# Layer 2: query projections moved into the recurrence's flow, low-rank projections beside the values, bonus as a thread

## The chip, the cores and the metric

One core of a Trainium2 chip runs the whole two-layer network in one launch. The metric is the device time of a run in microseconds (us). TensorE (PE) does the matmuls, VectorE (DVE) and ScalarE (ACT) and GpSimd (POOL) the elementwise work, and SyncE (SP) issues all the DMAs from one queue.

## The reference

The network is a backbone over 256 context and 512 latent tokens of width 1024. Layer 1 (mLSTM and GLA heads) and the two ConvFFNs are not touched. Layer 2 is bidirectional RWKV-7 time mixing. Six blends of the input `h` with its shifted version feed six projections; then a recurrence runs over the tokens in both directions, for 16 heads of 64:

```python
def rwkv_project(h, shifted, mu, w_rkv, w0, w1, w2, a0, a1, a2, g1, g2, kvec):
    xx = shifted - h
    xr, xw, xk, xv, xa, xg = (h + xx * mu[i] for i in range(6))
    r = xr @ w_rkv[0]
    k = xk @ w_rkv[1]
    v = xv @ w_rkv[2]
    lw = jnp.einsum("zblr,zrd->zbld", jnp.tanh(jnp.einsum("bld,zdr->zblr", xw, w1)), w2) + w0[:, None, None, :]
    decay = jnp.exp(-jnp.exp(-jax.nn.softplus(-lw.astype(jnp.float32)) - 0.5))
    a = jax.nn.sigmoid(a0 + (xa @ a1) @ a2)
    g = jax.nn.sigmoid(xg @ g1) @ g2
    ...
def step(S, inp):
    rt, wt, kt, vt, kkt, at = inp
    sa = jnp.einsum("bhvk,bhk->bhv", S, -kkt)
    S = S * wt[:, :, None, :] + sa[..., None] * (kkt * at)[:, :, None, :] + vt[..., None] * kt[:, :, None, :]
    return S, jnp.einsum("bhvk,bhk->bhv", S, rt)
def rwkv_out(y, p, kvec, lnx, w_o):
    r, k, v, g = p["r"], p["k"], p["v"], p["g"]
    y = head_layernorm(from_heads(y), lnx[0], lnx[1], RW_HEADS, r.dtype)
    bonus = jnp.sum((r * k * kvec[2]).reshape(...), axis=-1, keepdims=True) * v.reshape(...)
    return ((y + bonus.reshape(bn, L, D)) * g) @ w_o
```

Only the latent tokens leave layer 2, so `r` and `g` are needed for 512 tokens; `k`, `v`, `a` and the decay for all 768.

## The kernel before

The channels lie on the partitions: an activation is eight tiles of 128 x 768 (columns 0 to 255 context, `CT`; 256 to 767 latent). A dense projection of one block of 128 outputs ("unit") takes, for each of the eight input chunks, three matmuls: activations and weights are split into a rounded high part and a rest, and high x high, low x high and high x low are summed. `unit` loads 512 KB of weights (`wraw`), lets ScalarE round them (`whi`), and VectorE or GpSimd subtract (`wlo`). `variant` makes a blend: VectorE `vt = xx * mu + h`, ScalarE the high part, VectorE the rest.

On-chip tiles come from one pool of 41 slots of 128 x 780 (`sl`), the weights from 15 slots, PSUM has eight banks. A scheduler below the kernel takes the instructions by their order in the program, but lets a later one go first when it is ready and a slot is free, and gives every slot and wait.

Layer 2's mixer (`rwkv_mixer`) has two parts. The first is written in a fixed order: the shifted differences `xx` (eight tiles; `hf` holds the input); the values (`first("v", ...)` for units 0 to 3, `rkv(2, ...)` for 4 to 7), with two steps of the decay's low-rank projection (`lowrank(1, ...)`, into `uw`) behind each of the last four; then the queries (`pairs(0, CT)`, `first("r", ...)`, `rkv(0, ...)`), with steps of the low-rank projections of `a` (into `ua`) and of the gate (into `ug`) behind them, as the list `LOWS` says. Values and queries go to DRAM (`dv`, `dq`).

The second part is a planner's order. `flow` runs some hundred generators ("threads") and always advances the one that can start first by the times that `Meter` reckons for each instruction; it knows the engines and the PSUM banks, not the 41 slots. What a generator yields is a wait: a name is another thread's end, `"@2"` two banks. The threads, for each pair `p` of heads and each unit `u = 2p + z` (`z` the direction):

- `kp{p}`: the key projection (`kproj`; its variants by `pairs(2, 0)`, the last use of `xx` and `hf`);
- `shared{p}`: `kk`, `a`, the corrected `k`, stored to DRAM (`dkk`, `dP`); it also loads `r` and `v` and works out the bonus, `dbv`;
- `load{p}`: brings `kk`, `P0`, `P1`, `r` back (waits for the last key projection);
- `decay{u}`, `prep{u}`, `past{u}` (stretches of `rwkv_prep`: the products `T1` of a unit and its `dx` in DRAM), `leaf{u}` (inverse of 16 x 16 blocks on VectorE, there and back through DRAM: `dx`, `dqi`, `q0t`), `feed{u}`, `trans{g}_{u}` (TensorE: the chunks' transition matrices, `pmg`, `pmy`, `pmt`), `rec{u}` (the chain over 12 chunks, `cst`);
- `close{p}`: layer norm, bonus, gate; `wo` and `fill` (the modulation projection of the next blocks, `mfill`) take up gaps.

Of the kernel before, what the change touches and what calls it, by code (L numbers as in the profile page):

```python
# [18 lines left out]
P = 128  # L19
# [217 lines left out]
def flow(meter, threads):  # L237

    done, waiting, ready, engine = {}, {}, [], {}
    for i, (name, g) in enumerate(threads):
        ready.append((0.0, i, name, g, 0))

    def place(g):
        while hasattr(g.gi_yieldfrom, "gi_frame"):
            g = g.gi_yieldfrom
        return g.gi_code.co_name, g.gi_frame.f_lineno if g.gi_frame else 0

    def when(e):  # L250

        return max(e[0], meter.free.get(engine.get(place(e[3])), 0.0)), not e[2].startswith("rec"), e[0], e[1]
    while ready:
        e = min(ready, key=when)
        ready.remove(e)
        t, i, name, g, n = e
        if n:
            b = meter.banks(n)
            if b is None:
                waiting.setdefault("@", []).append(e)  # L260
                continue
            if b > t:
# [36 lines left out]
POST_LAG = 0  # L299
UP_TAGS = ({"C": "CCRR", "L": "LLRR"}, {"L": "LRCR"})  # L300
UP_FIRST = 2
LOWS = (0, 0, 1, 2, 2, 1, 1, 1)
RKV_TAGS = dict(v={"C": "CCRR", "L": "LLRR"}, r={"L": "LL"}, k={"L": "L", "C": "C"})


class Net:
# [971 lines left out]
    def rwkv_mixer(self, hf, xd, norms=None, post=lambda *a: None):  # L1278
# [15 lines left out]
        for seg in (CTX, LAT):  # L1294
            if norms is not None:
                next(norms)
            staggered([enter(j, seg) for j in range(NC)])
        uw, ua, ug = self.sl("uw"), self.sl("ua"), self.sl("ug", LT)
        nc.gpsimd.memset(ua[64:128], 0.0)
        dv = self.dr.tile([P, NC, T], F32, name="dv")  # L1300
        dq = self.dr.tile([P, NC, LT], F32, name="dq")

        def store(p, pst, d, segs):
            o = min(s[0] for s in segs)
# [8 lines left out]
        def pairs(i, o):  # L1313
            vh, vl = self.pairs("v")
            staggered([self.variant(i, j, xx, hf, vh, vl, o, T) for j in range(NC)])
            return vh, vl

        def first(which, n, d, segs, vh, vl):
            tags = RKV_TAGS[which]
            psts = self.proj2([I["rkv"][n, p] for p in range(len(tags["L"]))], vh, vl, segs, tags)  # L1320
            for p, pst in enumerate(psts):
                store(p, pst, d, segs)

        def kproj():
# [4 lines left out]
            for p in range(NC):  # L1329
# [14 lines left out]
        def evac_g(o, w, ps):  # L1344
            nc.scalar.activation(ug, ps, AF.Tanh, scale=0.5)
            nc.vector.tensor_scalar(ug, ug, 0.5, 0.5, op0=ALU.mult, op1=ALU.add)
        first("v", 2, dv, (CTX, LAT), vh, vl)
        low = self.lowrank(1, I["rw1"], xx, hf, SEGS, P, "R", lambda o, w, ps: nc.scalar.activation(uw[:, o:o + w], ps, AF.Tanh))
        for p in range(4, NC):
            rkv(2, p, dv, SEGS, vh, vl)  # L1350
            drain(part(low, 2))
        next(low)
        vh, vl = pairs(0, CT)
        low = [self.lowrank(4, I["ra1"], xx, hf, SEGS, 64, "R", lambda o, w, ps: nc.scalar.copy(ua[0:64, o:o + w], ps)),
               self.lowrank(5, I["rg1"], xx, hf, (LAT,), P, "R", evac_g)]
        first("r", 0, dq, (LAT,), vh, vl)
        for p in range(len(RKV_TAGS["r"]["L"]), NC):
            rkv(0, p, dq, (LAT,), vh, vl)
            for g in low:
                drain(part(g, LOWS[p]))  # L1360
        for g in low:
            next(g)
        dz = self.dr.tile([P, NC, LT], F32, name="dz")
        small = (uw, ua, ug, blk, half)
        st = [dict(dirs=[{}, {}], ys=[None]) for _ in range(NC)]
        zh, zl, y = [None] * NC, [None] * NC, []
        meter = self.nc = Meter(nc)
# [27 lines left out]
        def prep(u):  # L1395
            p, z = divmod(u, 2)
            if u:
                yield f"decay{u - 1}"
            yield f"load{p}"
            yield from self.rwkv_prep(p, z, st[p], uw, half, [f"trans{g}_{u - 3}" for g in range(3)] if u > 2 else [])  # L1400

        def leaf(u):
            yield f"prep{u}"
# [26 lines left out]
        def shared(p):  # L1430
            yield f"kp{p}"
            if p > 1:
                yield f"shared{p - 2}"
            yield from self.rwkv_shared(p, dv, dq, small, st[p])

        def load(p):
            yield f"kp{NC - 1}"
            yield f"shared{p}"
            if p:
                yield f"decay{2 * p - 2}"  # L1440
            if p > 1:
                for g in range(3):
                    yield f"trans{g}_{2 * p - 4}"
            self.rwkv_load(p, dq, st[p])
# [30 lines left out]

        preps = [prep(u) for u in range(2 * NC)]
        threads = [(f"kp{p}", kpart(p)) for p in range(NC)] + [(f"shared{p}", shared(p)) for p in range(NC)]
        for u in range(2 * NC):
            p, z = divmod(u, 2)
            threads += [(f"load{p}", load(p))] if z == 0 else []  # L1480
            threads += [(f"decay{u}", stretch(u, "decay")), (f"prep{u}", stretch(u, "prep", "decay")), (f"past{u}", stretch(u, "past", "prep")), (f"leaf{u}", leaf(u)), (f"feed{u}", feed(u))]
            threads += [(f"values{p}", values(p))] if z == 0 else []
# [3 lines left out]
        flow(meter, threads + [("wo", early()), ("fill", self.mod_fill(1, range(4, 12)))])  # L1486
        self.nc = nc
        ss = self.sums(WO_SUMS)
        xc = self.rload(xd, CT)
# [5 lines left out]
        post(y, H1, xc, ss, zh, zl)()  # L1495
        return zh, zl

    def rwkv_shared(self, p, dv, dq, small, st):


        nc, I = self.nc, self.I
# [59 lines left out]
        r, v = self.sl("r", LT), self.sl("v", LT)  # L1561
        nc.sync.dma_start(r, dq[:, p, :])
        nc.sync.dma_start(v, dv[:, p, CT:T])
# [4 lines left out]
        nc.sync.dma_start(dP[0][B], k[B])  # L1568
        nc.sync.dma_start(dP[1][A], k[A])

        nc.vector.scalar_tensor_tensor(r, r, self.v("kvec", 16 + p, 1), k[:, CT:T], op0=ALU.mult, op1=ALU.mult)
        yield True
        yield "@1"
        pb = self.take("pbo")
# [5 lines left out]
        st["dbv"] = self.dr.tile([P, LT], F32, name=f"dbv{p}")  # L1580
        nc.sync.dma_start(st["dbv"], v)

    def rwkv_load(self, p, dq, st):
# [9 lines left out]
        for n, d, w in (("kk", st["dkk"], T), ("P0", st["dP"][0], T), ("P1", st["dP"][1], T), ("r", dq[:, p, :], LT)):  # L1593
            st[n] = self.sl(n, w)
            nc.sync.dma_start(st[n], d)

# [47 lines left out]
    def rwkv_prep(self, p, z, st, uw, half, room):  # L1644
# [1 line left out]


        nc = self.nc
        P0, P1, kk, r, w2 = (st[n] for n in ("P0", "P1", "kk", "r", "w2"))
# [39 lines left out]
        nc.gpsimd.tensor_tensor(ri[:, :, 64:128], c64(r), eL[:, 4:12, e:e + 64], op=ALU.mult)  # L1689

        G3 = lambda t, g: c64(t)[:, 4 * g:4 * g + 4]
        T1 = []
# [453 lines left out]
```

## Time and profile before

| | us |
|---|---|
| median of 3 runs | 2759.9 (2747.04 to 2769.5) |
| profiled execution, its own time | 2768.18 |
| its span in the profile | 2766.2 |
| mean granted TensorE clock | 0.939 of full speed |
| TensorE busy | 2529.3 (91%) |
| TensorE weight loads busy | 2040.7 (74%) |
| VectorE / ScalarE / GpSimd busy | 1605.3 / 1057.3 / 970.0 |

The profile is a page of totals (busy time of the engines, 40 slices of the span, the DMA queues, the costliest groups of instructions) and views that can be asked of any stretch. A row of a stretch reads: from:to in us, length, then busy time with the count of instructions for PE, PEld (weight loads), DVE, ACT, POOL, then the granted clock, the DMA engines' busy share and GB/s. A group reads: line, engine, operation, output<-inputs, shape, count | busy us, mean ns | idle time of the engine ahead of it and what ended it. Many lines of the flow show as L233, since its helper issues every operation; there one goes by the tiles' names (`pk` keys, `pjL` values and queries, `prL` low-rank, `pbo` bonus, `ps` prep's products).

### The profile page before, as it was taken

The page shows a single profiled execution, that of the slowest core. Times are in us where ns is not written, and L with a number is a line of the kernel's source. Part 1 is how long each engine was busy: PE and PEld are TensorE (multiplying, and loading weights), DVE is VectorE, ACT ScalarE, POOL GpSimd, SP SyncE. Part 2 cuts the span into 40 slices and gives each one's busy share as a digit, 9 for nine tenths or more (in the row PEclk, how much of TensorE's full clock was granted, in tenths as well). Part 3 has the DMA queues.
Part 4 walks back from the last instruction along what each step waited for, and adds up shares of the span by engine and source line. Part 5 has one row for each costly group of instructions (what it writes and reads, how often), then busy time and mean ns, then how long its engine had stood idle before and what let it go on. Part 6 is the DMA issues. An engine that isn't in the chain of part 4 may idle for free. (4 is left out here: it accounts for less than half of the span.)

```text
span 2766.2 us, 47123 instructions
## 1 busy us (share of the span) xinstructions
PE 2529.3 (91%) x18916; PEld 2040.7 (74%) x18916; DVE 1605.3 (58%) x2915; ACT 1057.3 (38%) x2205; POOL 970.0 (35%) x1031
## 2 busy tenths in 40 slices
PE   5889999878899999997989879999999998799998
PEld 2677777767888888886756647576768777678886
DVE  4567757734554464747465374665565554676774
ACT  4543443444333232334343233433443443443332
POOL 2443355444222322246212251322222212344425
PEclk8999999998899999997999989999999998899999
DMA  6221234341212212132234453333322222333323
GB/s 226 73 83 60 70 106 146 99 159 52 78 54 59 87 37 78 54 126 73 90 109 151 153 135 80 89 86 98 86 45 65 47 69 85 107 92 94 90 84 107
DMA packets 195667, 254.57 MB, mean 92 GB/s; under 512 B 112120, under 2 KB 127864, under 8 KB 195448
## 3 DMA queue, kind: packets, MB, share of 16 engines
q1 hardware_dynamic: 195448, 251.56, 30.2%
q8 instruction: 149, 2.44, 0.4%
q14 instruction: 70, 0.57, 0.1%
HBM read 213.61 MB, written 37.89 MB: 91 GB/s over the span
## 5 line engine op out<-in xcount | busy, mean ns | idle before, releaser
L397 POOL TENSOR_TENSOR wlo<-wraw,whi 128x512 fp32r<-128x512 f32 (+1 forms) x393 | 543.2, 1404 | 890.7 <-ACT whi L220 454.8
L1123 DVE SCALAR_TENSOR_TENSOR fa<-pl,vec,fa 128x512 f32<-128x512 f32 x352 | 331.3, 948 | 181.4 <-ACT fa L220 175.0
L233 POOL TENSOR_SCALAR_AFFINE_SELECT T<-T 64x256 f32<-64x256 f32 x192 | 98.3, 514 | 270.9 <-ACT T L233 227.4
L220 ACT CAST whi<-wraw 128x512 fp32r<-128x512 f32 (+1 forms) x288 | 149.3, 581 | 68.0 <-DMA wraw<-in_up 26.2
L396 ACT CAST whi<-wraw 128x512 fp32r<-128x512 f32 x241 | 139.0, 619 | 74.0 <-DMA wraw<-in_wmod 22.2
L397 DVE TENSOR_TENSOR wlo<-wraw,whi 128x512 fp32r<-128x512 f32 x136 | 115.5, 887 | 77.8 <-ACT whi L220 34.0
L220 ACT COPY pl<-pjL 128x512 f32<-128x512 f32 x44 | 25.8, 586 | 339.4 <-PE pjL L412 304.0
L408 PE MATMUL pjL<-zh,whi 128*128 128x512 f32 x320 | 126.2, 394 | 2.2 <-ACT whi L220 2.2
L409 PE MATMUL pjL<-ml,whi 128*128 128x512 f32 x320 | 126.6, 396 | 0.0
L409 PE MATMUL pjL<-zl,whi 128*128 128x512 f32 x320 | 126.3, 395 | 0.0
L412 PE MATMUL pjL<-zh,wlo 128*128 128x512 f32 x320 | 126.1, 394 | 0.1
L408 PE MATMUL pjL<-mh,whi 128*128 128x512 f32 x320 | 126.1, 394 | 0.0
L412 PE MATMUL pjL<-mh,wlo 128*128 128x512 f32 x320 | 126.0, 394 | 0.0
L233 DVE TENSOR_SCALAR SU<-cst,el 64x64 f32<-64x64 f32 x176 | 51.1, 291 | 116.2 <-PE cst L233 113.1
L412 PE MATMUL pdL<-gh,wlo 128*128 128x512 f32 x288 | 113.8, 395 | 1.0 <-POOL wlo L397 1.0
L408 PE MATMUL pdL<-gh,whi 128*128 128x512 f32 x288 | 113.3, 394 | 0.2 <-ACT whi L220 0.2
L409 PE MATMUL pdL<-gl,whi 128*128 128x512 f32 x288 | 113.2, 393 | 0.0
L1175 DVE TENSOR_TENSOR y<-y,pdL 128x512 f32<-128x512 f32 x48 | 33.0, 687 | 108.3 <-PE pdL L412 108.2
L233 PE MATMUL pmy<-T,q0t 64*64 64x192 f32 x768 | 94.1, 349 | 0.8 <-DVE SU L233 0.8
L233 ACT ACTIVATE SU<-cst,el 64x64 f32<-64x64 f32 x176 | 53.6, 307 | 104.1 <-PE cst L233 103.6
L233 PE MATMUL ps<-bk,av 64*64 64x192 f32 x768 | 89.5, 355 | 3.5 <-DVE bk L233 1.9
L408 PE MATMUL pjC<-mh,whi 128*128 128x256 f32 x320 | 89.8, 281 | 0.0
(502 smaller groups left out, 7328.1 us busy)
## 6 DMA issues: line engine op xcount, KB each, us to landing
wraw<-in_up SPq DMA_DIRECT2D x88, 512.0 KB, 3.6
wraw<-in_wmod SPq DMA_DIRECT2D x64, 512.0 KB, 4.0
wfill<-in_wmod SPq DMA_DIRECT2D x32, 512.0 KB, 5.1
wraw<-in_rkv SPq DMA_DIRECT2D x24, 512.0 KB, 3.8
wraw<-in_win_fm SPq DMA_DIRECT2D x21, 512.0 KB, 4.4
wraw<-in_down SPq DMA_DIRECT2D x32, 320.0 KB, 2.9
xd<-y SPq DMA_DIRECT2D x64, 128.0 KB, 1.8
wraw<-in_down SPq DMA_DIRECT2D x32, 256.0 KB, 2.6
```

What stands on the lines that cost most here:

```text
L220: return lambda *a, **k: self.tc.keep_in_program_order(f(*a, **k))
L233: return f(*a, **k)
L396: nc.scalar.copy(hi[:, c], raw[:, c])
L397: (nc.gpsimd if lo == "pool" else nc.vector).tensor_tensor(w[:, c], raw[:, c], hi[:, c].bitcast(F32), op=ALU.subtract)
L408: nc.tensor.matmul(pst[tag][:m, :w], w1, xh[kc][:, o:o + w], start=st, stop=False)
L409: nc.tensor.matmul(pst[tag][:m, :w], w1, xl[kc][:, o:o + w], start=False, stop=False)
L412: nc.tensor.matmul(pst[tag][:m, :w], w0, xh[kc][:, o:o + w], start=False, stop=sp)
L1123: nc.vector.scalar_tensor_tensor(b, src, fw(f, i), b, op0=ALU.mult, op1=ALU.add)
L1175: nc.vector.tensor_tensor(yj, yj, pst[tag][:, :w], op=ALU.add)
```

## The change

- The query stage leaves the fixed order. At the mixer's start, 16 DMAs store the latent columns of `hf` and `xx` in DRAM (`dhx`). In the flow, after the last key projection, two threads (`rvar0`, `rvar1`) load them back a chunk at a time and make the query variants; threads `rp{p}` do the query units, two at a time, and store each in a DRAM tile of its own (`dq[p]`); `rload{p}` brings it back. `prep` takes `r` after its decay part and waits for `rload` there; unit 2's decay waits for the last query unit.
- The gate's low-rank projection becomes a thread, `gates`, after the last query unit, with loads and variants of its own; `close` waits for it.
- The low-rank projection of `a` moves to the values: units 4 and 5 carry four steps each of the decay's, 6 and 7 four steps each of `a`'s.
- The bonus leaves `rwkv_shared` and is a thread, `bonus{p}`, after `prep{2p}`; it loads `r`, `v` and the two halves of `k` from DRAM. `close` waits for it.
- `flow` learns a signal within a thread: a yield of `"!3"` marks the step as done under the thread's name with that mark.

```diff
@@ flow
+        elif isinstance(x, str) and x[0] == "!":
+            done[name + x] = t = max(t, meter.end)
+            ready += [(max(t, t2), *r) for t2, *r in waiting.pop(name + x, ())]
+            ready.append((t, i, name, g, 0))
@@ rwkv_mixer
-        uw, ua, ug = self.sl("uw"), self.sl("ua"), self.sl("ug", LT)
+        dhx = [self.dr.tile([P, 2, LT], F32, name=f"dhx{j}") for j in range(NC)]
+        for j in range(NC):
+            nc.sync.dma_start(dhx[j][:, 0], hf[j][:, CT:T])
+            nc.sync.dma_start(dhx[j][:, 1], xx[j][:, CT:T])
+        uw, ua = self.sl("uw"), self.sl("ua")
...
+        def latent(i, chunks, use):
...
+            for n, j in enumerate(chunks):
+                for e in chunks[n:n + 2]:
+                    if e not in src:
+                        src[e] = self.sl("hx", LT), self.sl("hx", LT)
+                        for q in range(2):
+                            nc.sync.dma_start(src[e][q], dhx[e][:, q])
+                h, x = src[j]
+                hi, lo = self.sl("rh", LT, F32R), self.sl("rl", LT, F32R)
+                yield True
+                nc.vector.scalar_tensor_tensor(x, x, self.v("mu", i * 8 + j, 1), h, op0=ALU.mult, op1=ALU.add)
...
+                nc.scalar.copy(hi, x)
...
+                nc.vector.tensor_tensor(lo, x, hi.bitcast(F32), op=ALU.subtract)
+                yield True
+                use(j, hi, lo)
+                yield f"!{j}"
...
+        def rpart(p, rh, rl, us):
...
+            us[p] = self.unit(I["rkv"][0, p], "pool" if p % 2 else "dve")
+            yield "@1"
+            ps = self.take("pr")
+            for j in range(NC):
+                yield f"rvar{j % 2}!{j}"
+                for k, (a, b) in enumerate(((0, rh), (0, rl), (1, rh))):
+                    nc.tensor.matmul(ps, us[p][a][:, j * P:(j + 1) * P], b[j], start=j + k == 0, stop=j == NC - 1 and k == 2)
+                yield False
...
+            nc.sync.dma_start(dq[p], t)
...
         for p in range(4, NC):
             rkv(2, p, dv, SEGS, vh, vl)
-            drain(part(low, 2))
-        next(low)
-        vh, vl = pairs(0, CT)
...
-        first("r", 0, dq, (LAT,), vh, vl)
-        for p in range(len(RKV_TAGS["r"]["L"]), NC):
-            rkv(0, p, dq, (LAT,), vh, vl)
-            for g in low:
-                drain(part(g, LOWS[p]))
...
+            drain(part(low[(p - 4) // 2], 4))
+            if p % 2:
+                next(low[(p - 4) // 2])
@@ prep
+            if u == 2:
+                yield f"rp{NC - 1}"
             yield f"load{p}"
-            yield from self.rwkv_prep(p, z, st[p], uw, half, [f"trans{g}_{u - 3}" for g in range(3)] if u > 2 else [])
+            yield from self.rwkv_prep(p, z, st[p], uw, half, ([f"trans{g}_{u - 3}" for g in range(3)] if u > 2 else []) + [f"rload{p}"])
@@ threads
+        def queries(p):
+            yield f"kp{NC - 1}"
+            if p > 1:
+                yield f"rp{p - 2}"
+            yield from rpart(p, rh, rl, rus)
+
+        def variants(i):
+            yield f"kp{NC - 1}"
...
+            yield from latent(0, range(i, NC, 2), use)
+
+        def gates():
+            yield f"rp{NC - 1}"
+            yield from gproj()
+
+        def bonus(p):
+            yield f"prep{2 * p}"
+            if p:
+                yield f"bonus{p - 1}"
+            yield from self.rwkv_bonus(p, dv, dq[p], blk, st[p])
...
+        def rload(p):
+            yield f"rp{p}"
+            yield f"load{p}"
+            st[p]["r"] = self.sl("r", LT)
+            self.nc.sync.dma_start(st[p]["r"], dq[p])
+            yield True
...
         def close(p):
             yield f"rec{2 * p + 1}"
+            yield f"bonus{p}"
+            yield "gates"
@@ rwkv_bonus (was in rwkv_shared)
+        r, v, k = (self.sl(n, LT) for n in ("r", "v", "k"))
+        nc.sync.dma_start(r, dq)
+        nc.sync.dma_start(k[A], st["dP"][1][A, CT:T])
+        nc.sync.dma_start(k[B], st["dP"][0][B, CT:T])
+        nc.sync.dma_start(v, dv[:, p, CT:T])
+        yield True
+        nc.vector.scalar_tensor_tensor(r, r, self.v("kvec", 16 + p, 1), k, op0=ALU.mult, op1=ALU.mult)
```

More of the change, by code (lines that the diff above doesn't have):

```diff
@@ L301 @@
 UP_FIRST = 2
-LOWS = (0, 0, 1, 2, 2, 1, 1, 1)
-RKV_TAGS = dict(v={"C": "CCRR", "L": "LLRR"}, r={"L": "LL"}, k={"L": "L", "C": "C"})
+RKV_TAGS = dict(v={"C": "CCRR", "L": "LLRR"})
 class Net:
@@ L1297, in rwkv_mixer @@
             staggered([enter(j, seg) for j in range(NC)])
-        uw, ua, ug = self.sl("uw"), self.sl("ua"), self.sl("ug", LT)
+        dhx = [self.dr.tile([P, 2, LT], F32, name=f"dhx{j}") for j in range(NC)]
[3 more added lines that the diff above has]
+        uw, ua = self.sl("uw"), self.sl("ua")
         nc.gpsimd.memset(ua[64:128], 0.0)
         dv = self.dr.tile([P, NC, T], F32, name="dv")
-        dq = self.dr.tile([P, NC, LT], F32, name="dq")
+        dq = [self.dr.tile([P, LT], F32, name=f"dq{p}") for p in range(NC)]
         def store(p, pst, d, segs):
@@ L1343, in kproj @@
                 yield "next"
-        def evac_g(o, w, ps):
+        def latent(i, chunks, use):
+            nc = self.nc
+            src = {}
+            for n, j in enumerate(chunks):
[15 more added lines that the diff above has]
+                yield f"!{j}"
@@ L1345, in evac_g, with gproj, use @@
+        def gproj():
+            nc = self.nc
+            wg = self.unit(I["rg1"])
+            yield "@1"
+            ps = self.take("prg1")
+            def use(j, hi, lo):
+                for k, (a, b) in enumerate(((0, hi), (0, lo), (1, hi))):
+                    nc.tensor.matmul(ps, wg[a][:, j * P:(j + 1) * P], b, start=j + k == 0, stop=j == NC - 1 and k == 2)
+            yield from latent(5, range(NC), use)
+            yield True
             nc.scalar.activation(ug, ps, AF.Tanh, scale=0.5)
+            self.close(ps)
+            yield True
@@ L1346, in evac_g @@
             nc.vector.tensor_scalar(ug, ug, 0.5, 0.5, op0=ALU.mult, op1=ALU.add)
+        def rpart(p, rh, rl, us):
+            nc = self.nc
+            us[p] = self.unit(I["rkv"][0, p], "pool" if p % 2 else "dve")
+            yield "@1"
+            ps = self.take("pr")
[4 more added lines that the diff above has]
+                yield False
+            yield True
+            t = self.sl("pr", LT)
+            nc.scalar.copy(t, ps)
+            self.close(ps)
+            yield True
+            nc.sync.dma_start(dq[p], t)
@@ L1347, in rwkv_mixer @@
         first("v", 2, dv, (CTX, LAT), vh, vl)
-        low = self.lowrank(1, I["rw1"], xx, hf, SEGS, P, "R", lambda o, w, ps: nc.scalar.activation(uw[:, o:o + w], ps, AF.Tanh))
+        low = [self.lowrank(1, I["rw1"], xx, hf, SEGS, P, "R", lambda o, w, ps: nc.scalar.activation(uw[:, o:o + w], ps, AF.Tanh)),
+               self.lowrank(4, I["ra1"], xx, hf, SEGS, 64, "R", lambda o, w, ps: nc.scalar.copy(ua[0:64, o:o + w], ps))]
         for p in range(4, NC):
             rkv(2, p, dv, SEGS, vh, vl)
-            drain(part(low, 2))
@@ L1352, in rwkv_mixer @@
-        next(low)
-        vh, vl = pairs(0, CT)
-        low = [self.lowrank(4, I["ra1"], xx, hf, SEGS, 64, "R", lambda o, w, ps: nc.scalar.copy(ua[0:64, o:o + w], ps)),
-               self.lowrank(5, I["rg1"], xx, hf, (LAT,), P, "R", evac_g)]
-        first("r", 0, dq, (LAT,), vh, vl)
-        for p in range(len(RKV_TAGS["r"]["L"]), NC):
-            rkv(0, p, dq, (LAT,), vh, vl)
-            for g in low:
-                drain(part(g, LOWS[p]))
-        for g in low:
-            next(g)
+            drain(part(low[(p - 4) // 2], 4))
@@ L1363, in rwkv_mixer @@
+            if p % 2:
+                next(low[(p - 4) // 2])
         dz = self.dr.tile([P, NC, LT], F32, name="dz")
+        ug = self.sl("ug", LT)
         small = (uw, ua, ug, blk, half)
+        rh, rl, rus = [None] * NC, [None] * NC, {}
         st = [dict(dirs=[{}, {}], ys=[None]) for _ in range(NC)]
@@ L1433, in shared, with use @@
                 yield f"shared{p - 2}"
-            yield from self.rwkv_shared(p, dv, dq, small, st[p])
+            yield from self.rwkv_shared(p, small, st[p])
+        def queries(p):
[5 more added lines that the diff above has]
+            yield f"kp{NC - 1}"
+            def use(j, hi, lo):
+                rh[j], rl[j] = hi, lo
+            yield from latent(0, range(i, NC, 2), use)
[7 more added lines that the diff above has]
+            yield from self.rwkv_bonus(p, dv, dq[p], blk, st[p])
         def load(p):
@@ L1443, in load @@
                     yield f"trans{g}_{2 * p - 4}"
-            self.rwkv_load(p, dq, st[p])
+            self.rwkv_load(p, st[p])
+            yield True
+        def rload(p):
[3 more added lines that the diff above has]
+            self.nc.sync.dma_start(st[p]["r"], dq[p])
             yield True
@@ L1477, in rwkv_mixer @@
         threads = [(f"kp{p}", kpart(p)) for p in range(NC)] + [(f"shared{p}", shared(p)) for p in range(NC)]
+        threads += [(f"rvar{i}", variants(i)) for i in range(2)] + [(f"rp{p}", queries(p)) for p in range(NC)]
         for u in range(2 * NC):
             p, z = divmod(u, 2)
-            threads += [(f"load{p}", load(p))] if z == 0 else []
+            threads += [(f"load{p}", load(p)), (f"rload{p}", rload(p))] if z == 0 else []
             threads += [(f"decay{u}", stretch(u, "decay")), (f"prep{u}", stretch(u, "prep", "decay")), (f"past{u}", stretch(u, "past", "prep")), (f"leaf{u}", leaf(u)), (f"feed{u}", feed(u))]
-            threads += [(f"values{p}", values(p))] if z == 0 else []
+            threads += [(f"values{p}", values(p)), (f"bonus{p}", bonus(p))] if z == 0 else []
             threads += [(f"trans{g}_{u}", trans(u, g)) for g in ((0, 1, 2), (0, 2, 1))[z]]
@@ L1485, in rwkv_mixer @@
             threads += [(f"close{p}", close(p))] if z else []
-        flow(meter, threads + [("wo", early()), ("fill", self.mod_fill(1, range(4, 12)))])
+        flow(meter, threads + [("gates", gates()), ("wo", early()), ("fill", self.mod_fill(1, range(4, 12)))])
         self.nc = nc
@@ L1496, in rwkv_mixer, with rwkv_shared @@
         return zh, zl
-    def rwkv_shared(self, p, dv, dq, small, st):
+    def rwkv_shared(self, p, small, st):
         nc, I = self.nc, self.I
@@ L1560, in rwkv_shared @@
         nc.sync.dma_start(dP[1][B], q[B])
-        r, v = self.sl("r", LT), self.sl("v", LT)
-        nc.sync.dma_start(r, dq[:, p, :])
-        nc.sync.dma_start(v, dv[:, p, CT:T])
         nc.vector.tensor_scalar(a, a, -1.0, self.v("kvec", 8 + p, 1), op0=ALU.add, op1=ALU.mult)
@@ L1569, in rwkv_shared, with rwkv_bonus @@
         nc.sync.dma_start(dP[1][A], k[A])
-        nc.vector.scalar_tensor_tensor(r, r, self.v("kvec", 16 + p, 1), k[:, CT:T], op0=ALU.mult, op1=ALU.mult)
+    def rwkv_bonus(self, p, dv, dq, blk, st):
+        nc = self.nc
+        A, B = slice(0, 64), slice(64, 128)
+        r, v, k = (self.sl(n, LT) for n in ("r", "v", "k"))
[3 more added lines that the diff above has]
+        nc.sync.dma_start(v, dv[:, p, CT:T])
+        yield True
+        nc.vector.scalar_tensor_tensor(r, r, self.v("kvec", 16 + p, 1), k, op0=ALU.mult, op1=ALU.mult)
         yield True
@@ L1581, in rwkv_shared, with rwkv_load @@
         nc.sync.dma_start(st["dbv"], v)
-    def rwkv_load(self, p, dq, st):
+    def rwkv_load(self, p, st):
         nc, I = self.nc, self.I
@@ L1592, in rwkv_load @@
         st["w2"] = w2[:, 0], w2[:, 1]
-        for n, d, w in (("kk", st["dkk"], T), ("P0", st["dP"][0], T), ("P1", st["dP"][1], T), ("r", dq[:, p, :], LT)):
+        for n, d, w in (("kk", st["dkk"], T), ("P0", st["dP"][0], T), ("P1", st["dP"][1], T)):
             st[n] = self.sl(n, w)
@@ L1648, in rwkv_prep @@
         nc = self.nc
-        P0, P1, kk, r, w2 = (st[n] for n in ("P0", "P1", "kk", "r", "w2"))
+        P0, P1, kk, w2 = (st[n] for n in ("P0", "P1", "kk", "w2"))
         C6 = math.exp(-0.5)
@@ L1688, in rwkv_prep @@
         nc.vector.scalar_tensor_tensor(av, c64(kk), -1.0, eL[:, :, z:z + 64], op0=ALU.mult, op1=ALU.mult)
-        nc.gpsimd.tensor_tensor(ri[:, :, 64:128], c64(r), eL[:, 4:12, e:e + 64], op=ALU.mult)
+        nc.gpsimd.tensor_tensor(ri[:, :, 64:128], c64(st["r"]), eL[:, 4:12, e:e + 64], op=ALU.mult)
         G3 = lambda t, g: c64(t)[:, 4 * g:4 * g + 4]
```

## The prediction, made before the change was run

> **What bounds the kernel now.** I read the page first (busy shares, the 40 slices), then cut layer 2 into stages with the view that gives busy time by stretches, then looked inside two of them with the groups, the waits and the order of time.
>
> ```profile
> PE 2529.3 (91%) x18916; PEld 2040.7 (74%) x18916; DVE 1605.3 (58%) x2915; ACT 1057.3 (38%) x2205; POOL 970.0 (35%) x1031
> core 0: us, PE busy (x) PEld busy (x) DVE busy (x) ACT busy (x) POOL busy (x), PEclk, DMA share, GB/s
> 1342.00:1386.00 44.00, 42.13 (x239) 36.01 (x237) 20.40 (x22) 16.96 (x30) 12.84 (x9) 1.00 0.42 148
> 1386.00:1459.00 73.00, 65.34 (x268) 44.32 (x267) 44.72 (x56) 29.89 (x50) 9.35 (x7) 1.00 0.33 106
> 1459.00:1575.00 116.00, 112.22 (x594) 83.75 (x592) 46.05 (x68) 34.92 (x60) 35.52 (x28) 0.99 0.42 136
> 1575.00:1670.00 95.00, 69.56 (x481) 42.67 (x480) 68.14 (x164) 28.81 (x57) 42.87 (x67) 0.78 0.62 166
> 1670.00:2320.00 650.00, 626.45 (x8327) 478.56 (x8324) 354.01 (x969) 258.56 (x630) 163.77 (x310) 0.95 0.30 75
> ```
>
> The five rows are the stages the change touches: values 4 to 7 with the decay low-rank projection; queries with the other two low-rank projections; keys (the first part of the planner's flow); the start of the recurrence; its long remainder. TensorE is the busiest engine, and four rows show it full or nearly so. The fourth does not. In those 95 us it is busy 69.6 us, at a granted clock of 0.78, so it does about 69.6 x 0.78 = 54 us of full-clock work: **some 41 us are spare**. Nothing else with so much room is near. Where the hole is:
>
> ```profile
> 1575.00:1585.00 10.00, 5.61 (x19) 1.98 (x17) 5.03 (x6) 3.08 (x6) 3.95 (x5) 0.95 0.88 263
> 1585.00:1595.00 10.00, 4.94 (x6) 1.67 (x6) 5.24 (x8) 1.58 (x2) 1.18 (x1) 0.50 0.93 344
> 1655.00:1665.00 10.00, 2.54 (x18) 2.07 (x19) 7.83 (x31) 0.00 (x0) 2.25 (x5) 0.53 1.11 196
> PE pmg L233 <- DMA q0t<-dqi: 8.8, 1, 8.8
> PE pbo L233 <- DVE r L233: 8.6, 2, 5.4
> 1461.73 0.97 PE L233 MATMUL pk<-vh,whi 128*128 128x512 f32 x4 [0.51 <-ACT vh L233]
> 1573.94 0.52 PE L233 MATMUL pk<-vh,wlo 128*128 128x512 f32 x2
> 1662.46 0.45 PE L233 MATMUL pmg<-q0t,T 64*64 64x64 f32 x2 [8.80 <-DMA q0t<-dqi]
> 1592.06 1.18 POOL L233 TENSOR_TENSOR ri<-r,eL 128x512 f32<-128x512 f32 x1 [13.11 <-ACT eL L233]
> ```
>
> The keys run from 1461.7 to 1574.4; then two pieces follow. When the last key projection ends, everything runs on loads (DMA 0.9 busy) and on the bonus's `r`; later the first `trans` waits for the leaf inverse's trip through DRAM. Both are latency: a chain load, prep, T1, leaf, q0t that nothing shortens, with too little TensorE work beside it: 88 us from the last key matmul to the first `trans`. The change brings TensorE work (the query projections) to exactly this stretch, so the question is how much of it fits.
>
> **The change part by part, on the profiled execution (2768.2 us).** The shown runs' median, 2759.9 us, is 8.3 us below it, inside their spread; I carry the difference over.
>
> *The query stage goes from the fixed order.* Its contents:
>
> ```profile
> L408 PE MATMUL pjL<-vh,whi 128*128 128x512 f32 x48 | 19.0, 397 | 0.5 <-ACT pv L1307 0.5
> L435 PE MATMUL pjL<-vl,whi 128*128 128x512 f32 x16 | 7.1, 446 | 0.3 <-DVE vl L1254 0.3
> L409 PE MATMUL prL<-rl,whi 128*128 128x512 f32 x8 | 3.8, 473 | 1.4 <-DVE rl L1254 1.4
> L409 PE MATMUL prL<-rl,whi 128*64 128x512 f32 x8 | 3.3, 412 | 3.0 <-DVE rl L1254 3.0
> 1430.73 0.39 PE L408 MATMUL prL<-rh,whi 128*128 128x512 f32 x1
> 1430.96 0.40 PE L408 MATMUL pjL<-vh,whi 128*128 128x512 f32 x1
> 1431.19 0.39 PE L409 MATMUL pjL<-vl,whi 128*128 128x512 f32 x1
> ```
>
> Each group has two sisters (high x high, low x high, high x low), so queries are 3 x (48 + 16) = 192 matmuls of 512 columns, the gate projection 24, the `a` projection 24 plus 24 of 256 columns. The starts in order of time are 0.23 us apart though each lasts 0.39 (they overlap), so I count 0.233 us a piece: queries 44.7 us, gate 5.6, `a` 5.6 + 2.8 = 8.4. Together 58.7 of the stage's 73, the rest is waiting for variants. Term: **-73.0**.
>
> *The `a` projection moves beside the values.* +8.4 us on TensorE. The values' stretch then carries 16 low-rank steps for 8; the query stage lost 73 - 58.7 = 14.3 us over its entry and 16 steps, under 0.9 a step, so eight more cost 0 to 7; I take 4, since the values' stretch with its eight steps lost only 1.9 us. **+12.4**. The keys' entry is as before: their variants wait for the last projection's slots in both orders.
>
> *Queries and gates in the flow.* 44.7 + 5.6 = **+50.3** on TensorE if nothing hides. The spare 41 us of the hole take most: **-40.7**. But the work isn't there at once. Their input is now 16 loads of 256 KB (16 more for the gates), variants are computed again, and `r` goes out and back:
>
> ```profile
> L1251 DVE SCALAR_TENSOR_TENSOR vt<-xx,vec,y 128x512 f32<-128x512 f32 x15 | 12.1, 808 | 1.3 <-DMA dq<-pv 1.1
> L1252 ACT CAST vh<-vt 128x512 fp32r<-128x512 f32 x8 | 4.9, 618 | 8.9 <-DVE vt L1251 8.9
> L1254 DVE TENSOR_TENSOR vl<-vt,vh 128x512 fp32r<-128x512 f32 x8 | 5.5, 691 | 6.1 <-ACT vh L1252 6.1
> L397 DVE TENSOR_TENSOR wlo<-wraw,whi 128x512 fp32r<-128x512 f32 x4 | 2.6, 687 | 5.9 <-DMA dq<-pv 5.9
> r<-dq SPq DMA_DIRECT2D x16, 256.0 KB, 4.6
> dq<-pv SPq DMA_DIRECT2D x8, 256.0 KB, 3.6
> ```
>
> The first variant is ready 4.6 + 0.81 + 0.62 + 0.69 = 6.7 us after its loads are issued, and they are issued when the last key projection frees the bank of slots; eight need 8 x (0.81 + 0.69) = 12 us of VectorE. Query 0 is thus done some 25 us into the stretch (6.7, the 12, and a share of VectorE's other work: an estimate), and reaches prep 0 about 3.6 + 4.6 us and a copy (0.6) later. Its `ri` now waits that long (before: 18 us in); the trip is hidden from TensorE by queries 1 to 7 (39 us of matmuls), not from the chain. VectorE carries 68 us in 95 already and gets 12 of variants and 4 x 2 x 0.69 = 5.5 of weight halves: still under its span. Then slots: 41 tiles, of which query variants hold 16 and `uw`, `ua`, `ug`, `zero` 4, so unit 1's preparation comes behind query 7 and the second hole (7.5 us idle, the rest at 0.53) stays in part. Not hidden: 6.7 at the head, and about 15 near the first `trans`, twice that hole's idle: **+22**. Ends: 0, if loads and variants are hoisted into the key stage, and 41, if nothing fits.
>
> *Bonus a thread.* Its work (2 matmuls, two VectorE passes a pair) leaves the start and comes later, with four loads and one store a pair.
>
> ```profile
> L233 PE MATMUL pbo<-r,blk 128*128 128x512 f32 x8 | 6.1, 878 | 8.6 <-DVE r L233 8.6
> L233 PE MATMUL mfill<-wfill,cth 128*2 128x512 f32 x23 | 12.1, 633 | 0.0
> ```
>
> On TensorE 16 matmuls, at most 2 x 6.1 = 12 us; the remainder has 650 - 626 x 0.95 = 55 us spare and takes them: 0, up to +12 if that cover is gone. The modulation filler (23 in the hole) is off the path: displaced pieces go to later gaps; up to +12 if none takes them. So -6 (a lighter start) to +24 for both, I take 0, the row nearest being the 55 spare.
>
> *Sixteen stores of the two inputs.* They are issued when the shifted input is done:
>
> ```profile
> 1310.00:1320.00 10.00, 2.58 (x6) 1.95 (x7) 10.00 (x14) 3.38 (x6) 6.90 (x7) 0.50 0.00 0
> 1330.00:1340.00 10.00, 10.00 (x45) 8.17 (x44) 0.04 (x1) 0.70 (x2) 0.00 (x0) 1.00 0.00 0
> dbv<-v SPq DMA_DIRECT2D x8, 256.0 KB, 2.0
> ```
>
> The DMA engines do nothing there and the values' first weights are in: 4 MB at the 344 GB/s seen above is 12 us of an empty queue. 0; were the stores to block SP ahead of the next weights, up to +6.
>
> **Sum:** -73.0 + 12.4 + 50.3 - 40.7 + 22 = **-29.0**: 2739 for the profiled execution, 2731 against the median.
>
> **Rivals.**
>
> *Nothing fits (2760).* The query threads begin only after the last key; they delay prep 0 as much as they fill, and the spare time is still there behind them. Then -73 + 12.4 + 50.3 + 8.8 for the trip of `r` = -1.5. For it: the 16 + 8 slots, VectorE at 72% in the hole. Against: queries 1 to 7 need no answer from anybody.
>
> *It fits altogether (2709).* The 22 us left are taken by the key stage (early loads) and by the remainder: -51.
>
> ```profile
> PE cst L233 <- DVE SU L233: 10.5, 19, 2.1
> ```
>
> For it: the remainder's 55 us, of which TensorE's waits (the longest group above) are only part. The Trainium skill ("Perfetto Trace Analysis", Identifying the Most-Contended Engine) says that matmul occupancy is no good measure of TensorE's headroom and that the weight loads' busy share is better; by that rule the remainder has room for another 25%, not 4%, and all the moved work could hide there. The trace has 479 of 650 us for weight loads, but no row shows which of the two is right. Against: the matmuls there are small and many, and no wait is long.
>
> *Slower: the SP queue (2793).* SP issues in order, and the remainder hangs on it:
>
> ```profile
> 1642.72 0.45 SPq L233 DMA_DIRECT2D dqi<-leaf  x1
> 1649.26 5.32 SPq L233 DMA_DIRECT2D dx<-T  x6
> 1656.55 2.62 SPq L233 DMA_DIRECT2D q0t<-dqi  x2
> ```
>
> `q0t` left 13.8 us after the store it depends on, behind `dx` stores that waited for ScalarE, and `trans` paid 8.8. Now the bonus's store (which waits VectorE, TensorE and a slot) and its loads, `r`'s load and the gates' 16 loads stand in that queue in every pair. Where one is ahead of `q0t` or `kk`, `P0`, the pair pays up to 8.8 us: from 4 pairs on (35 us) the gain is gone, at 7 (62) it is -29 + 62 = +33. For it: the slots are scarcer too. Against: TensorE's longest waits in the remainder are the recurrence's own steps (the row above), not a DMA.
>
> **How the numbers follow.** Forecast 0.45 (own range 2711 to 2751), nothing fits 0.22, altogether 0.15, slower 0.18. The range takes the whole forecast, the second, most of the third and half of the last: 2702 to 2788, with some 0.15 to 0.2 outside. About 1% (27.6 us) is what a measurement of this kernel can tell from no change, and the forecast lies on that line: 0.24 of it faster, 0.21 same. Faster 0.24 + 0.15 = 0.39; same 0.21 + 0.18 + 0.03 = 0.42; slower 0.04 + 0.15 = 0.19.
>
> **What would show it.** Keys begin about 60 us sooner (near 1401 for 1461) with the values' stretch some 12 us longer; `pr` matmuls at 0.23 apart from some 7 us behind the last `pk`, done within 60 us; first `pmg` after the last `pk` by 88 us (as now) to 110; granted clock over that stretch nearer 0.95 than 0.78; remainder near 650 us plus what gates and bonus add, with no DMA among TensorE's waits. **Wrong** would be made by: a clock still near 0.8 there (nothing fits); `q0t` or `r` among TensorE's longest waits (the queue); keys that start less than 50 us sooner, since the values' stretch then is bound by its 16 variants.

## The result, and the profile after

| | before | after |
|---|---|---|
| median | 2760.3 us (2747.0 to 2769.5) | 2734.4 us (2730.8 to 2738.1) |
| ratio to before | | 0.9904, 95% interval 0.9881 to 0.9926 |
| span of the profiled execution | 2766.2 | 2732.7 |

The changed kernel is faster by 26.5 us (20 to 33); the forecast was 2731. The profiled executions differ by 33.5 us, of which 6.6 arose ahead of the mixer: its first shifted input stands at 1277.0 before and at 1270.4 after, and in the fourteen traces of this case, with the same work ahead of it, that row lies anywhere from 1267.9 to 1277.0. Times inside the mixer are therefore given from that row on.

The tile views give, for each group of TensorE or GpSimd instructions, count, then duration min/median/max in ns, then start of the first and of the last. Of the kernel before (last keys, first `trans` and the last product of the output projection):

```profile
L1219 POOL TENSOR_TENSOR xx<-y x16: 603/925/1332, 1277.0 to 1315.0; 128x255 f32<-128x255 f32 x8, 128x504 f32<-128x504 f32 x4, 128x448 f32<-128x448 f32 x4
L233 PE MATMUL pk<-vh,wlo x128: 274/389/629, 1464.0 to 1574.2; 128*128 128x512 f32 x64, 128*128 128x256 f32 x64
L233 PE MATMUL pmg<-q0t,T x768: 216/218/367, 1662.5 to 2264.8; 64*64 64x64 f32 x192
L233 PE MATMUL wo<-zh,wlo x48: 387/396/628, 2254.5 to 2319.1; 128*128 128x512 f32 x48
```

And of the changed kernel, with the query units (`pr`):

```profile
L1222 POOL TENSOR_TENSOR xx<-y x16: 606/924/1336, 1270.4 to 1308.5; 128x255 f32<-128x255 f32 x8, 128x504 f32<-128x504 f32 x4, 128x448 f32<-128x448 f32 x4
L233 PE MATMUL pk<-vh,whi x128: 275/387/988, 1394.8 to 1500.5; 128*128 128x512 f32 x64, 128*128 128x256 f32 x64
L233 PE MATMUL pk<-vh,wlo x128: 274/387/628, 1397.1 to 1501.0; 128*128 128x512 f32 x64, 128*128 128x256 f32 x64
L233 PE MATMUL pr<-rh,wlo x64: 387/393/794, 1512.1 to 1619.3; 128*128 128x512 f32 x64
L233 PE MATMUL pmg<-q0t,T x768: 216/218/367, 1584.6 to 2225.9; 64*64 64x64 f32 x192
L233 PE MATMUL wo<-zh,wlo x48: 387/397/503, 2212.9 to 2283.1; 128*128 128x512 f32 x48
```

| from the first shifted input | before | after | change |
|---|---|---|---|
| first key matmul | 184.7 | 124.4 | -60.3 |
| last key matmul | 297.2 | 230.6 | -66.6 |
| first `trans` | 385.5 | 314.2 | -71.3 |
| last output product | 1042.1 | 1012.7 | -29.4 |

So 71 us are gained by the first `trans`, and 42 of them are given back behind it. The stages (columns as before: from:to, length, busy us of PE, PEld, DVE, ACT, POOL, granted clock, DMA share, GB/s):

```profile
1394.00:1501.00 107.00, 104.16 (x587) 83.36 (x586) 46.03 (x68) 37.63 (x65) 38.04 (x25) 0.98 0.42 129
1501.00:1585.00 84.00, 78.33 (x449) 51.80 (x448) 46.97 (x105) 29.89 (x56) 31.91 (x49) 0.95 0.68 203
1585.00:1630.00 45.00, 43.02 (x441) 29.88 (x440) 13.04 (x35) 12.17 (x26) 3.33 (x3) 0.86 0.39 121
1630.00:1710.00 80.00, 76.78 (x774) 49.56 (x774) 63.37 (x149) 37.04 (x86) 38.62 (x68) 0.98 0.45 121
1710.00:2285.00 575.00, 551.48 (x7371) 421.63 (x7370) 325.21 (x887) 227.15 (x554) 143.96 (x268) 0.96 0.34 87
PE pr L233 <- DVE rl L233: 3.0, 2, 2.9
PE mfill L233 <- ACT frow L233: 1.3, 2, 0.7
PE pmg L233 <- DVE leaf L233: 1.3, 1, 1.3
```

The hole is closed: 84 us from the keys to the first `trans` where it was 88, TensorE busy 78 of them at a clock of 0.95, spare 84 - 78.3 x 0.95 = 9.6 us. (The 95 us and the 41 spare of the prediction are of a stretch that runs 7.5 us past the first `trans`; from 1574 to 1662.5 TensorE was busy 63.1 us at 0.81, which leaves 37 spare.) The three last rows are TensorE's longest waits between 1501 and 1630; the 8.8 us on `q0t` are gone. That looks like a plain success of filling, and the experiments show that it isn't one.

### The profile page after: what moved, and what is told of

It reads as the page before. It is cut to its first block, busy times and chain, and to the rows that moved or that the text cites. A ratio compares the mean times of both kernels' runs of the same rounds, so it can differ in the third digit from the quotient of the medians.

```text
span 2732.7 us, 47246 instructions
## 1 busy us (share of the span) xinstructions
PE 2517.5 (92%) x18916; PEld 2031.1 (74%) x18916; DVE 1594.9 (58%) x2915; ACT 1056.1 (39%) x2205; POOL 974.7 (36%) x1031
## 5 line engine op out<-in xcount | busy, mean ns | idle before, releaser
L400 POOL TENSOR_TENSOR wlo<-wraw,whi 128x512 fp32r<-128x512 f32 (+1 forms) x383 | 528.5, 1402 | 836.9 <-ACT whi L220 468.5
L399 ACT CAST whi<-wraw 128x512 fp32r<-128x512 f32 x223 | 128.1, 618 | 56.7 <-DMA wraw<-in_wmod 24.2
L400 DVE TENSOR_TENSOR wlo<-wraw,whi 128x512 fp32r<-128x512 f32 x128 | 109.2, 891 | 65.5 <-ACT whi L220 34.3
L233 POOL TENSOR_TENSOR wlo<-wraw,whi 128x512 fp32r<-128x512 f32 (+1 forms) x26 | 34.7, 1348 | 158.1 <-ACT whi L233 121.7
```

The lines of the kernel that those rows point to most:

```text
L233: return f(*a, **k)
L399: nc.scalar.copy(hi[:, c], raw[:, c])
L400: (nc.gpsimd if lo == "pool" else nc.vector).tensor_tensor(w[:, c], raw[:, c], hi[:, c].bitcast(F32), op=ALU.subtract)
```

## The experiments

All ratios are to the kernel before, run on the same chip (medians 2759.7, 2762.5 and 2760.0 in the three groups of four). One per cent is 27.6 us.

| run | median us | ratio | 95% interval |
|---|---|---|---|
| the changed kernel | 2734.4 | 0.9904 | 0.9881 to 0.9926 |
| e1 queries in the fixed order | 2756.5 | 0.9991 | 0.9978 to 1.0004 |
| e2 no queries | 2693.5 | 0.9760 | 0.9747 to 0.9773 |
| e3 no gates | 2724.3 | 0.9869 | 0.9857 to 0.9882 |
| e4 before, `a` beside the values | 2765.5 | 1.0017 | 0.9998 to 1.0036 |
| e5 unit 2 without its wait | 2749.4 | 0.9958 | 0.9944 to 0.9972 |
| e6 queries preferred | 2726.4 | 0.9871 | 0.9852 to 0.9890 |
| e7 gates beside the values | 2726.5 | 0.9874 | 0.9854 to 0.9893 |
| e8 before, bonus a thread | 2760.0 | 0.9990 | 0.9975 to 1.0005 |
| e9 few query matmuls | 2735.4 | 0.9910 | 0.9878 to 0.9942 |
| e10 one variant pair | 2741.7 | 0.9934 | 0.9916 to 0.9952 |
| e11 e6 and e7 together | 2726.9 | 0.9875 | 0.9851 to 0.9899 |
| e12 e11, variants earlier | 2724.7 | 0.9873 | 0.9850 to 0.9896 |

**Which part of the change is it?** e1 undoes the queries' move alone:

```diff
...
+        vh, vl = pairs(0, CT)
+        first("r", 0, dq, (LAT,), vh, vl)
+        for p in range(2, NC):
+            rkv(0, p, dq, (LAT,), vh, vl)
         dz = self.dr.tile([P, NC, LT], F32, name="dz")
...
-            yield from rpart(p, rh, rl, rus)
+            return
...
-            yield from latent(0, range(i, NC, 2), use)
+            return
+            yield
```

> The query units go back to the fixed order behind the values (their variants from the on-chip input); gates, bonus and the a projection stay as in the changed kernel. Theory (the gain is TensorE work of the queries hidden in the start of the recurrence): the stage costs 44.7 us of matmuls and 4 to 5 of entry again, and the flow gives back the some 23 it pays for them, so about 2760 (2752 to 2767), with the stretch from the last key matmul to the first trans at a granted clock near 0.8 again. Rival (the gain comes from the other moves: a beside the values, bonus and gates out of the way): 2734, within 6.

It came out at 2756.5: nothing that can be told from the kernel before is left of the gain. In its trace the query stage is back, and so is the hole, with its clock:

```profile
1384.00:1447.00 63.00, 57.77 (x230) 38.57 (x228) 21.28 (x30) 22.60 (x40) 10.88 (x9) 1.00 0.42 135
1553.00:1647.00 94.00, 68.28 (x427) 40.23 (x425) 67.85 (x161) 31.42 (x59) 42.81 (x62) 0.83 0.65 177
```

The other moves were put on the kernel before one at a time. e4 gives the values the steps of both low-rank projections:

```diff
         for p in range(4, NC):
             rkv(2, p, dv, SEGS, vh, vl)
-            drain(part(low, 2))
-        next(low)
+            drain(part(low[(p - 4) // 2], 4))
+            if p % 2:
+                next(low[(p - 4) // 2])
...
```

> The kernel before, with only the a projection moved beside the values; queries and the gate's projection stay in the fixed order. Theory: TensorE work only changes places, and 8 waits of under 0.9 us become 8 of about half: 2757 (2750 to 2762). Rival (the low-rank projections behind the queries were the stall, and this move is the gain): 2745 or less.

e8 takes the bonus out of `rwkv_shared` into its thread:

```diff
+        def bonus(p):
+            yield f"prep{2 * p}"
+            if p:
+                yield f"bonus{p - 1}"
+            yield from self.rwkv_bonus(p, dv, dq[:, p, :], blk, st[p])
...
             yield f"rec{2 * p + 1}"
+            yield f"bonus{p}"
...
```

> The kernel before with only the bonus made a thread. Theory: its work moves out of the stretch between the keys and the first trans, which waits on loads anyway, into the remainder, which has room: 2758 (2750 to 2766). Rival (its waits on loads at the start were part of the hole): 2750 or less.

Neither moves the time beyond the noise: +4.7 us (-0.6 to +9.9) and -2.8 us (-6.9 to +1.4). So the gain belongs to the queries' move. What each way of doing them costs is seen against a kernel without them, e2:

```diff
...
-            yield from rpart(p, rh, rl, rus)
+            return
...
+        for d in dq:
+            nc.sync.dma_start(d, zero[:, 0:LT])
...
```

> The query units and their variants are left out (r is zero, stored once); everything else as in the changed kernel. Theory: only the part of the queries that isn't hidden goes, some 23 us: 2711 (2702 to 2718). Rival (nothing of them is hidden, they only changed places): their 44.7 us of matmuls and more go, 2688 or less.

2693.5: **the queries cost 63 us in the fixed order (2756.5 - 2693.5) and 40 us in the flow (0.9904 - 0.9760 = 1.44%)**, with 44.7 us of matmuls in both. Here the theory's number, 23, failed, and the time fell between the two that were expected: next to nothing of the 44.7 is hidden in the flow. What the move saved is mainly the rest of the fixed stage, some 18 us beyond its matmuls. Yet e2's trace has the same hole, open:

```profile
1499.00:1591.00 92.00, 68.32 (x426) 40.18 (x424) 67.88 (x160) 31.43 (x59) 42.07 (x62) 0.82 0.67 179
1591.00:1640.00 49.00, 49.00 (x659) 36.73 (x660) 20.03 (x45) 18.98 (x45) 9.66 (x19) 0.92 0.39 97
```

Its first `trans` comes 92 us behind the last key, the changed kernel's 84 us, so the queries don't delay it. But the two stretches don't hold the same work. From the last key to the first `trans` TensorE runs, in e2 (first row) and in the changed kernel:

```profile
L233 PE MATMUL ps<-ri,bk 64*64 64x128 f32 x96 | 6.6, 288 | 0.0
L233 PE MATMUL ps<-ri,bk 64*64 64x128 f32 x64 | 3.8, 269 | 0.0
L233 PE MATMUL pr<-rh,whi 128*128 128x512 f32 x48 | 19.9, 436 | 0.0
```

A unit has 32 of the first kind. e2, like the kernel before, has made the products of three units by its first `trans`, the changed kernel of two. Its 144 query matmuls (the last row and two sisters) took in part the place of the third unit, which comes behind.

**Is unit 2's wait the price?** The third `ri` (the step of `prep` that uses `r`) shows when the third unit is made; the GpSimd rows in order of time, of e2:

```profile
1517.40 1.18 POOL L233 TENSOR_TENSOR ri<-r,eL 128x512 f32<-128x512 f32 x1
1538.73 1.18 POOL L233 TENSOR_TENSOR ri<-r,eL 128x512 f32<-128x512 f32 x1
1560.72 1.56 POOL L233 TENSOR_TENSOR ri<-r,eL 128x512 f32<-128x512 f32 x1 [0.39 <-POOL T L233]
```

and of the changed kernel:

```profile
1544.81 1.18 POOL L233 TENSOR_TENSOR ri<-r,eL 128x512 f32<-128x512 f32 x1
1552.16 1.73 POOL L233 TENSOR_TENSOR ri<-r,eL 128x512 f32<-128x512 f32 x1
1639.50 1.70 POOL L233 TENSOR_TENSOR ri<-r,eL 128x512 f32<-128x512 f32 x1 [1.02 <-ACT eL L233]
```

Counted from the last key matmul (1498.9 and 1501.0) the third unit is 77 us later, behind the last query (1619). e5 takes the wait out:

```diff
-            if u == 2:
-                yield f"rp{NC - 1}"
```

> The changed kernel, but unit 2's decay doesn't wait for the last query unit (its load and slots still gate it). Theory (the queries are free up to the first trans, and then cost some 30 us because unit 2, which starts 64 us later than in the run without queries, leaves the recurrence without its third unit): unit 2's first matmul comes before 1600 us, the third rec ends 15 to 25 us sooner, and the time falls by 8 to 20: 2720. Rival (the 41 slots, not the wait, hold unit 2 back: 16 are the query variants'): no change within 5, or slower.

The kernel became slower by 15 us. In its profiled execution (2760.3 us, the slowest of ten) the third `ri` came 72 us behind the last key instead of 138, the first `trans` 96 us instead of 84. SP waited for the leaf inverse's tiles 37.5 us in the stretch from 1500 to 1720, where the changed kernel has 11.7:

```profile
SPq L233 <- DVE leaf L233: 37.5, 8, 14.5
SPq L233 <- DVE leaf L233: 11.7, 6, 8.4
```

(the second row is the changed kernel's). So the wait isn't a fault. That it keeps a third unit off the tiles and the queue that the first two need is the likely reason, not a shown one: e2 has its third unit as early, and SP waits there 18.7 us. e6 moves the end of the queries instead: the planner prefers them.

```diff
-        return max(e[0], meter.free.get(engine.get(place(e[3])), 0.0)), not e[2].startswith("rec"), e[0], e[1]
+        return max(e[0], meter.free.get(engine.get(place(e[3])), 0.0)), not e[2].startswith(("rec", "rp", "rvar")), e[0], e[1]
```

> The changed kernel, but the planner prefers the query threads, as it does the recurrence's chain, where two could start at once; so the queries end sooner and units 0 and 1 are made later. Theory (unit 2's late start is the price): the last query matmul comes 20 us or more before 1619, unit 2 follows, and the time falls by 5 to 15: 2724. Rival (the price is TensorE time, which only changes hands): within 5 of 2734; if the first trans is later by as much as the queries are sooner, slower by up to 10.

2726.4, faster by about 9 us (0.9871 against 0.9904, the intervals overlap a little). Counted from the last key, the last query matmul came 48 us sooner (71 for 118) and the third unit's `ri` 37 us sooner (102 for 138), but the first `trans` 36 us later (120 for 84). Shifts of that size come down to 9 at the end. So the third unit's place is not the price by itself: 72 us behind the last key in e5, 102 in e6 and 138 in the changed kernel went with 2749, 2726 and 2734.

**TensorE's time, or what surrounds it?** e9 keeps everything of the queries but the matmuls, of which a few small ones remain; e10 keeps all the matmuls and takes away 14 of the 16 slots, 14 loads and seven variants.

```diff
-                for k, (a, b) in enumerate(((0, rh), (0, rl), (1, rh))):
-                    nc.tensor.matmul(ps, us[p][a][:, j * P:(j + 1) * P], b[j], start=j + k == 0, stop=j == NC - 1 and k == 2)
+                for k, (a, b) in enumerate(((0, rh), (0, rl))[:1 + (p == NC - 1)]):
+                    nc.tensor.matmul(ps[:, :128], us[p][a][:, j * P:(j + 1) * P], b[j][:, :128], start=j + k == 0, stop=j == NC - 1 and k == (p == NC - 1))
...
```

> The changed kernel with its loads, variants, weights, copies and slots, but of a query unit's 24 matmuls of 512 columns only 8 of 128 columns are left (16 in the last unit); r is wrong. Theory (what the queries still cost in the flow, 41 us by the run without them, is TensorE's time: the idle time that they fill comes back further on): nearly all of it goes, 2700 (2693 to 2708). Rival (the price is what surrounds them: 16 slots, loads, VectorE, the late r): 2718 or more.

```diff
-                yield f"rvar{j % 2}!{j}"
+                yield "rvar0!0"
...
-                    nc.tensor.matmul(ps, us[p][a][:, j * P:(j + 1) * P], b[j], start=j + k == 0, stop=j == NC - 1 and k == 2)
+                    nc.tensor.matmul(ps, us[p][a][:, j * P:(j + 1) * P], b[0], start=j + k == 0, stop=j == NC - 1 and k == 2)
...
-            yield from latent(0, range(i, NC, 2), use)
+            yield from latent(0, range(1 - i), use)
```

> The changed kernel with all its query matmuls, but all read one pair of variant tiles, made from one chunk (14 loads, 7 variants and 14 slots fewer); r is wrong. Theory (TensorE's time): 2730 (2722 to 2736). Rival (the slots and the loads): 2715 or less.

Neither gave anything: e9's 2735.4 agrees with its rival, e10's 2741.7 lies above what its theory and its rival expected. With 120 of 192 query matmuls gone and the other 72 at 128 columns for 512, the time is the changed kernel's. In e9's stretch behind the keys the hole is open again and TensorE idle, to no avail (first two rows); in e10 TensorE is full there (third row), the first `trans` is the earliest of all with queries in the flow, 73 us behind the last key, and the end isn't earlier:

```profile
1500.00:1595.00 95.00, 71.60 (x418) 46.84 (x416) 62.94 (x118) 37.84 (x70) 45.76 (x58) 0.80 0.73 220
1595.00:1640.00 45.00, 41.38 (x543) 32.22 (x545) 21.95 (x54) 16.29 (x38) 7.47 (x19) 0.89 0.52 125
1500.00:1595.00 95.00, 93.75 (x671) 63.91 (x672) 50.69 (x118) 32.33 (x62) 35.55 (x49) 1.00 0.57 163
```

What e9 does and doesn't show is seen in the whole stretch from the last key to the last output product, of e2, the changed kernel and e9:

```profile
1498.90:2247.00 748.10, 705.90 (x8824) 524.74 (x8823) 435.95 (x1151) 292.19 (x693) 209.46 (x374) 0.94 0.38 98
1501.00:2283.10 782.10, 747.71 (x9016) 551.02 (x9015) 448.08 (x1171) 305.34 (x719) 217.82 (x387) 0.95 0.39 105
1505.50:2285.30 779.80, 723.11 (x8896) 537.69 (x8895) 451.59 (x1171) 305.60 (x717) 222.57 (x383) 0.93 0.40 104
```

The changed kernel takes 34 us more than e2, with TensorE 42 us busier and 8 us less idle: the moved matmuls lengthen the flow by nearly their own time. In e9 TensorE is 25 us less busy than in the changed kernel and 22 us more idle, and the stretch is as long. So the theory that **TensorE's time alone is the price fails**: taking the matmuls out doesn't give it back. Nor do the matmuls count as hidden; something else in the flow takes as long without them. The slots, loads and variants that e10 took out aren't that by themselves.

What e9 and e10 have in common with the changed kernel, and e2 has not, are the eight weight units (load, ScalarE's rounding, the rest on VectorE or GpSimd), the queries' results, which are copied out and stored before a pair's load of `r` can start (e2 loads `r` too, but zeros stored early), the waits for the query threads, and the places that the planner gives to everything by them. Which of these does it **stays open**: no run took away the weight units or the late `r` alone, and every edit gives the planner another order.

**The gates, and a better version.** e3 leaves the gates' thread out, e7 moves their projection to the values, where the input is still on the chip:

```diff
-            yield from gproj()
+            nc.gpsimd.memset(ug, 0.5)
+            yield True
```

> The gates thread is left out (the gate is a constant 0.5): 24 matmuls, 16 loads, 8 variants. Theory: 5.6 us of TensorE and a little waiting go, 2726 (2720 to 2732). Rival (rebuilding an input from DRAM inside the recurrence is dear, through the SP queue and the slots): 2714 or less.

```diff
...
-               self.lowrank(4, I["ra1"], xx, hf, SEGS, 64, "R", lambda o, w, ps: nc.scalar.copy(ua[0:64, o:o + w], ps))]
+               self.lowrank(4, I["ra1"], xx, hf, SEGS, 64, "R", lambda o, w, ps: nc.scalar.copy(ua[0:64, o:o + w], ps)),
+               self.lowrank(5, I["rg1"], xx, hf, (LAT,), P, "R", evac_g)]
+        low = chain(*low)
...
-            drain(part(low[(p - 4) // 2], 4))
-            if p % 2:
-                next(low[(p - 4) // 2])
+            drain(part(low, 7))
...
```

> The changed kernel with the gate's low-rank projection in the fixed order beside the values too (24 steps behind values 4 to 7, on-chip input; no gates thread, no 16 loads). Theory: the flow saves the 10 us that leaving the gates out saved, the values' stretch pays 5.6 of matmuls and up to 4 of waiting: 2734 within 5. Rival (the rebuilt input is the dear part of the gates): 2727 or less.

e3: 2724.3, so the gates cost 10 us in the flow (0.9904 - 0.9869), as the theory had it within 2. e7: 2726.5, about 8 us faster than the changed kernel, at the edge of the noise; the time is the rival's. But the rival's reason, that the second trip is dear and the matmuls are not, isn't shown. The traces have the last key 236.9 us behind the first shifted input in e7 and 230.0 in e3: beside the values the gates paid some 7 us, as the theory expected. The flow behind it, from the last key to the last output product, took 762.6 us in e7, 773.0 in e3 and 782.1 in the changed kernel. That it is 10 us shorter in e7 than where the gates are left out altogether is unexplained.

e11 joins e6 and e7, e12 lets the variants start a key unit earlier:

```diff
         def variants(i):
-            yield f"kp{NC - 1}"
+            yield f"kp{NC - 2}"
```

> The gate's projection beside the values and the query threads preferred, together. If their 8 us each are of different causes (24 matmuls, loads and variants out of the flow; the order of units), they add: 2718 (2712 to 2724). If both only ease the same stretch behind the first trans: 2726.

> As the run before it, and the query variants may begin after the seventh key unit instead of the eighth. The head of the query stretch (some 7 us of little work behind the last key) is then covered: 4 to 7 us less than that run, 2713. If the slots are the bound there, as in the run without unit 2's wait: no less, or more.

2726.9 and 2724.7: the two gains don't add, and the earlier start adds nothing that can be measured. e7, the plainest of the four, is as good as any: 35 us (30 to 40) below the kernel before.

## Why the prediction was right, and where its steps were not

- **The fixed order** (-73.0 + 12.4 = -60.6). Keys began 60.3 us sooner. Right, so the values' stretch paid what was counted.
- **Keys' stage** (0 to -6 for the bonus leaving it; 0 taken). It became 6.3 us shorter, from 112.5 to 106.2.
- **Flow, hole and remainder together** (+50.3 - 40.7 + 22 = +31.6). Measured: -6.3 in the keys, -4.7 from the last key to the first `trans` (88.3 to 83.6), +41.9 behind it: +30.9. The sum held; its **placing failed**. The 22 us were put at the head and near the first `trans`, which was to come after 88 to 110 us; it came after 84, and the loss lay behind it.
- **The step that failed** is "the spare 41 us of the hole take most: -40.7". The hole did take 144 of the 192 query matmuls, but the third unit's products left it for them. By leaving out, the queries cost 40 us in the flow (e2; 34 in the traces behind the last key) and the gates 10 (e3; 9 in the traces). So of the 50.3 us no more than 7 were hidden in the end, where the sum has 40.7 - 22 = 18.7.
- **Where the gain came from.** The queries' own stage cost 63 us (e1 against e2): 44.7 of matmuls and 18 more, where the sum had 14.3 of waiting for the whole stage. That 63 became 40 is the gain, 23 of 26.5; the rest is the net of the other moves and can't be told from noise. The sum came within 4 us partly by luck: the measured +30.9 is 34 and 9 for queries and gates, less 6.3 in the keys' stage and 6 by which the flow without both is shorter than before (748.1 - 9.1 = 739.0 for 744.9), two gains that the sum had at nothing.
- **Why the moved queries cost 40.** By TensorE's busy time their matmuls alone would do it, and by e9 they aren't needed for it. This stays open.
- **The queries' pace.** "Done within 60 us" was wrong: the last came 118 us behind the last key, since the planner mixes them with the first units; preferred in e6, they were done after 71.
- **The rivals.** *Nothing fits*: wrong in its signs, as the clock rose to 0.95 and the time fell; but its core, that the queries push out as much as they fill, is close to what e2 shows. *The SP queue*: TensorE waits for no DMA among its longest in the changed kernel, and the time refutes it. *Fits altogether*: refuted by the time, 2734 for 2709. The remark there on the Trainium skill's rule ("Perfetto Trace Analysis", Identifying the Most-Contended Engine: matmul occupancy doesn't measure headroom) agrees with e9, whose time is the changed kernel's though TensorE is busy 20 us less in the whole execution (2497.7 for 2517.5). The other half, room by the weight loads' share, isn't borne out: that share was 551 of 782 us in the flow, and what was moved there cost its time all the same.
- **The chances.** The time fell on the line of 1%, as forecast; the interval of 20 to 33 us shows that the measurement tells finer than that line.

## What to carry to other kernels

A stage's idle time is not a budget that moved work simply uses up: here the moved work took the place of other work, which then had to be done behind it. Measure a moved part by leaving it out in both places (63 and 40 us here), and take away its arithmetic and its surroundings separately, before calling either the price. If the time stays when the arithmetic is out, compare the engine's busy and idle time over the whole stretch: where the idle time has grown by as much as the busy time fell, another limit of the same length stands beside the engine.

## What the runs showed that was not expected

- Taking a wait out made the kernel slower by 15 us (e5), although the unit that waited came 67 us sooner by its third `ri`, counted from the last key.
- With 120 of the 192 query matmuls gone and the other 72 a quarter as wide, the time didn't change (2735.4 and 2734.4): from the last key on, TensorE was 25 us less busy and 22 us more idle.
